# A two-layer hybrid trunk on one core: three of five gate/up pairs by seven products beside a stream of plain jobs, and half of the weight sums by adding transfers

## The chip, the core and the metric

The kernel runs on 1 core of one Trainium2 chip. The metric is device time in microseconds (us) of one execution, smaller is better; the figure compared is the median of several runs. The profile is of one execution; its engines are PE (TensorE, matmuls), PEld (its weight loads), DVE (VectorE), ACT (ScalarE), POOL (GpSimd) and SP (which here only issues transfers).

## What is computed

Two layers act on an activation of 256 rows by 1024 channels. Each layer has a mixer (retention beside a state-space scan) and a feed-forward part; only the latter is touched in what it computes:

```python
def swiglu(h, w_gate_up, w_down):          # h is 256 x 1024, after an RMS norm
    gu = h @ w_gate_up                     # 1024 x 5632
    gate, up = jnp.split(gu, [D_FF], axis=-1)     # D_FF = 2816
    return (jax.nn.silu(gate) * up) @ w_down      # 2816 x 1024
```

Inputs, weights and output are float32.

## The kernel before

**One weight piece.** Every weight arrives as a piece of 128 x 1024 numbers, 512 KB, that `feeder` (L405) loads through SP's queue into a `raw` slot, of which there are four. `split_piece` makes two operands of it: ACT copies it into `wh`, rounded to the format that the matmuls take (L421), and DVE subtracts to get the rest, `wl` (L428). `wh` and `wl` have six slots each (`hlS`). The activation is split the same way, and a product is three matmuls (`mm3`): xh·wh, xh·wl and xl·wh (L444, L445, L446). Pieces take their slots strictly in a written order (`turn`): a piece that is late holds up all that come after it.

**The feed-forward part.** Gate and up have 2816 columns each, worked on in pairs of 512 gate columns and the 512 up columns that belong to them: pairs 0 to 4, and a joint job of the last 256 columns of both. A plain pair is two jobs, gate and up, of four pieces each; a job is 8 row blocks x 2 row halves of the activation x 3 matmuls. After a job comes its evacuation: ACT takes the silu of the gate, DVE multiplies by the up part (L214, `sil<-acc,sil`), PE transposes the product (L486, `tr<-cst,sil`) and ACT and DVE split it for w_down.

**Seven products.** Pairs 2 and 4 (`WINO`) are worked as a 2 x 2 block product in Winograd's form of Strassen's scheme: rows of the activation in two halves, the 1024 inner channels in two halves, gate and up as the two column blocks. Seven products of half the size replace eight. Each is 4 x 3 matmuls, so the pair has 84 in place of 96. It needs seven weight operands of two pieces each (14 splits in place of 8). Their names are 11, t1, t2, 22, t3, 21 and t4. 11, 12, 22, 21 are the weight blocks as loaded, and

```
t1 = 11 + 12     t2 = t1 + 22     t3 = 12 + 22     t4 = t2 + 21
```

up to signs that the activation's sums and the evacuation carry. Block 11 lies in a `raws` slot (two slots, shared with the mixer's `seg`) and becomes t1, t2 and t4 there, one after another: split 11, add, split t1, add, split t2, add, split t4. Only then is the slot free. Four sums of the activation (`plain`, `D`) are made once per layer. One weight sum, t3, is made by a transfer that adds what it reads from HBM to what lies in the slot (L330, issued by POOL); the other three are DVE additions (L214, `raws<-raws,raw`), of 128 x 1024 each.

**Order.** All instructions come from a planner (`Flow`), which keeps a list per engine and issues by a number (the job) and readiness, with its own costs; the engines then run their lists strictly in order. Before, jobs stand one after another: pair 0, pair 1, pair 2, pair 3, pair 4, joint, w_down.

**Slots in the mixer.** PSUM is in three pools: `acc` with four slots, `tr` with two, `sm` with two for the mixer's small products. `ca` and `cb`, two slots each, hold the mixer's rotary and convolution halves.

Of the kernel before, what the change touches and what calls it, by code (L numbers as in the profile page):

```python
# [181 lines left out]
def trunk_kernel(  # L182
# [7 lines left out]
    WINO, ADDED = (2, 4), ("t3",)  # L190
# [49 lines left out]
    accS, new_acc = pooled(accp, (P, 512), F32, "acc", 4)  # L240
    trS, new_tr = pooled(trp, (P, 512), F32, "tr", 2)
    smS, new_sm = pooled(smp, (P, 512), F32, "sm", 2)
# [31 lines left out]
    def next_turn():  # L274
        turns.append(Event())
        return len(turns) - 1

    def add_job(srcs):
        evs = []
        for src, k, n in srcs:  # L280
            ev = Event()
            evs.append(ev)
            specs.append((src, k, n, len(jobs), (rawS, new_raw), splitter(next_turn(), k, n, ev, len(jobs))))
        jobs.append(evs)

    PRODUCTS = ("11", "t1", "t2", "22", "t3", "21", "t4")

    def add_wino(w, n1, n2):

        job = len(jobs)  # L290
        evs = {q: [Event(), Event()] for q in PRODUCTS}
        turn = {(q, i): next_turn() for q in PRODUCTS for i in range(2)}
        held = {(q, i): Event() for q in ("11", "12", "22", "21") for i in range(2)}
        part = {q: [rows(w, k0 + 2 * i * P, 2, n0, 512)[0][0] for i in range(2)]
                for q, k0, n0 in (("11", 0, n1), ("12", 0, n2), ("22", D // 2, n2), ("21", D // 2, n1))}
        for q in part:
            for i in range(2):
                land = holder(held[q, i])
                if (q, i) == ("11", 1):
                    land = then(land, [wino_sums(i, job, evs, turn, held, part) for i in range(2)])  # L300
                specs.append(([part[q][i]], 2, 512, job, (segS, new_raw_seg) if q == "11" else (rawS, new_raw), land))
        jobs.append(evs)
# [17 lines left out]
    def wino_sums(i, job, evs, turn, held, part):  # L320
# [3 lines left out]
        def split(raw, q):  # L324
            wh, wl = yield from split_piece(raw, D, turn[q, i], pr)
            fl.set(evs[q][i], tuple(a.rearrange("p (k n) -> p k n", k=2) for a in (wh, wl)))
# [7 lines left out]
        def last(raw, q, sem):  # L334
            yield from split(raw, q)
            fl.release(sem)

# [3 lines left out]
        def plus(q, x, raw, src):  # L341

            if q in ADDED:
                yield from add(x, src)
            else:
                w = yield raw
                yield tt(D, pr, x, x, w, ALU.add)
            fl.set(used[q])

        def side(ev, q, *sums):  # L350
            raw = yield ev
            yield from split(raw, q)
# [4 lines left out]
        def third():  # L357
            raw = yield w12
            if "t1" not in ADDED:
                yield used["t1"]  # L360
            yield from plus("t3", raw, w22, "22")
            yield from last(raw, "t3", rawS)

        fl.spawn(side(w22, "22", *(q for q in ("t2", "t3") if q not in ADDED)))
        fl.spawn(third())
        fl.spawn(side(w21, "21", *(q for q in ("t4",) if q not in ADDED)))
# [7 lines left out]
        yield from last(x, "t4", segS)  # L374
# [11 lines left out]
    def fm_srcs(w, n0):  # L386
        return [rows(w, k0, 4, n0, 256) for k0 in range(0, D, 4 * P)]

# [23 lines left out]
    def split_piece(raw, m, turn, pr):  # L412

        if turn:
            yield turns[turn - 1]
        yield hlS
        fl.set(turns[turn])
# [6 lines left out]
        wh = yield Op("act", 0.833 * m + 92, split_h, pr)  # L424

# [8 lines left out]
    def splitter(turn, k, n, ev, job):  # L434
        def land(raw, landed):
            yield landed
            wh, wl = yield from split_piece(raw, k * n, turn, job - 0.7)
# [62 lines left out]

    def power(ms, n, pr, tag, bufs):
# [19 lines left out]
    class Norm:  # L521


        def __init__(self, w, sums=False):
            self.plain = [[Event() if sums else None for _ in range(NT)] for _ in range(2)]
            self.ops = {q: Event() for q in PRODUCTS}
# [52 lines left out]

        def drop(self):  # L580
            for i in range(2):
                self.xT.drop(i)
            for _ in range(4):
                fl.release(bigS["D"])
# [20 lines left out]
    at_job = [0]  # L605
    started = [False]

    def tm_jobs(xT, members, order):

        first = at_job[0]  # L610
        at_job[0] += len(members)
        acc, left = {}, {}
        for m, t, k in order:
# [15 lines left out]
            yield pe(3 * mm_cost(n), j + 0.5, emit)  # L629
# [3 lines left out]
            if k == 7:  # L633
                fl.spawn(post(t, acc[m, t], j))

    def tm_job(xT, post, n=512, kper=2, lead=0):

        return tm_jobs(xT, [(post, n, kper)], [(0, t, k) for t in range(NT) for k in range(lead)]
                       + [(0, t, k) for k in range(lead, 8) for t in range(NT)])
# [6 lines left out]
    def wino_job(norm, post):  # L646
# [4 lines left out]
        j = at_job[0]  # L651
        at_job[0] += 1
        evs = jobs[j]

        def product(q, box, first):
            xh, xl = yield norm.ops[q]
            if first:
                yield accS
            for k in range(4):
                wh, wl = yield evs[q][k // 2]  # L660

                def emit():
                    if first and k == 0:
                        box.append(new_acc())
                    mm3(box[0], xh[:, k, :], xl[:, k, :], wh[:, k % 2, :], wl[:, k % 2, :], first and k == 0, k == 3,
                        skip_group_check=box is u)
# [1025 lines left out]
```

## Time and profile before

| | us |
|---|---|
| three runs | 1280.19, 1282.22, 1283.87 (median 1282.22) |
| profiled execution, its own time | 1282.07 |
| its span, first to last instruction | 1280.3 |
| outside the span | 1.8 |
| DVE busy, ACT busy in the span | 931.6, 774.5 |
| feed-forward part, layer 0 | about 467 to 586 in the span |
| feed-forward part, layer 1 | about 1097 to 1215 in the span |

In a row of the timeline stand start, length, engine, line, operation, out<-in and shape, a count for merged rows, and in brackets the idle time before it with what ended it. A matmul's length is longer than the distance to the next one, since they overlap in the array, so PE's pace is read from the starts. The same holds for DVE and ACT, whose writes end after the next instruction has begun. DMA share is the mean busy share of the core's 16 DMA engines.

### The profile page before, as it was taken

The numbers are of one execution on the slowest core, as the hardware profiler recorded it, in microseconds if no ns is written. First come the engines' busy times: TensorE is split into PE (matmuls) and PEld (weight loads), VectorE is DVE, ScalarE is ACT, GpSimd is POOL, SyncE is SP. The second block draws the span as 40 slices with busy tenths as digits, with TensorE's granted clock in tenths as the row PEclk, the third lists the DMA queues.
The fourth block names the chain that finished last, engine by engine and source line by source line (L and its number), as shares of the span: only waits on it lengthen the run. The fifth ranks groups of instructions, "written<-read, shape, count | busy, mean of one in ns | idle before, by whom it ended". The sixth has DMA issues, their size and how long they took to land.

```text
span 1280.3 us, 17056 instructions
## 1 busy us (share of the span) xinstructions
PE 1268.4 (99%) x6276; PEld 1065.7 (83%) x6276; DVE 931.6 (73%) x1243; ACT 774.5 (60%) x1138; POOL 43.1 (3%) x65
## 2 busy tenths in 40 slices
PE   9999999999999999999999999999999999999997
PEld 7888888888888888888888988888888888888886
DVE  5875789778576678995468658879875756889943
ACT  5765676977375365674367556867954643766732
POOL 1000000000010000000010000000000000000000
PEclk9999999999999999999999999999999999999999
DMA  7757555556465456766466565555555554667751
GB/s 242 221 166 221 164 185 161 181 183 212 140 223 202 161 173 188 265 206 221 157 188 202 170 201 160 185 181 179 193 182 175 203 198 148 224 169 232 242 199 53
DMA packets 131191, 241.86 MB, mean 189 GB/s; under 512 B 7946, under 2 KB 60034, under 8 KB 130979
## 3 DMA queue, kind: packets, MB, share of 16 engines
q1 hardware_dynamic: 127458, 232.16, 55.0%
q0 software_dynamic: 3648, 8.61, 3.3%
q8 instruction: 49, 0.80, 0.2%
q14 instruction: 36, 0.29, 0.1%
HBM read 239.63 MB, written 1.11 MB: 188 GB/s over the span
## 4 chain that ended last, share of the span: by engine, by line
PE 89%; DVE 4%; DMA 3%; issue 2%; ACT 2%; SPq 0%; POOLq 0%; POOL 0%; DVEq 0%; ACTq 0%
PE acc L444 21%; PE acc L446 21%; PE acc L445 21%; PE acc L740 10%; PE acc L741 6%; PE tr L486 2%; DVE wl L428 2%; PE yps L1282 2%; PE acc L743 1%; DMA raw<-in_w_gate_up_dram 1%; ACT wh L421 1%; DMA raw<-in_w_down_dram 1%; DMA raw<-in_w_in_dram 1%; PE tr L1176 1%; PE ips L1269 1%
## 5 line engine op out<-in xcount | busy, mean ns | idle before, releaser
L428 DVE TENSOR_TENSOR wl<-raw,wh 128x1024 fp32r<-128x1024 f32 (+2 forms) x424 | 503.8, 1193 | 216.8 <-ACT wh L421 214.5
L421 ACT ACTIVATE wh<-raw 128x1024 fp32r<-128x1024 f32 (+2 forms) x424 | 434.6, 1034 | 285.9 <-PE acc L446 193.0
L444 PE MATMUL acc<-wh,xT 128*128 128x512 f32 (+1 forms) x816 | 317.1, 389 | 1.0 <-ACT wh L421 0.6
L445 PE MATMUL acc<-wl,xT 128*128 128x512 f32 (+1 forms) x816 | 311.7, 382 | 0.8 <-DVE wl L428 0.7
L446 PE MATMUL acc<-wh,xT 128*128 128x512 f32 (+1 forms) x816 | 311.6, 382 | 0.0
L740 PE MATMUL acc<-xT,wh 128*128 128x512 f32 x560 | 203.6, 401 | 0.0
L444 PEld LDWEIGHTS acc<-wh,xT 128*128 128x128 f32 x816 | 153.3, 188 | 28.9 <-ACT wh L421 1.0
L445 PEld LDWEIGHTS acc<-wl,xT 128*128 128x128 f32 x816 | 153.4, 188 | 28.8 <-DVE wl L428 1.9
L446 PEld LDWEIGHTS acc<-wh,xT 128*128 128x128 f32 x816 | 153.2, 188 | 28.7
L741 PE MATMUL acc<-xT,wl 128*128 128x256 f32 x640 | 167.1, 281 | 0.0
L741 PEld LDWEIGHTS acc<-xT,wl 128*128 128x128 f32 x640 | 120.9, 189 | 6.9
L740 PEld LDWEIGHTS acc<-xT,wh 128*128 128x128 f32 x560 | 105.4, 188 | 21.4
L444 PE MATMUL acc<-wh,A 128*128 128x512 f32 x192 | 76.6, 399 | 0.0
L217 DVE SCALAR_TENSOR_TENSOR cb<-ca,cv,cb 128x255 f32<-128x255 f32 (+1 forms) x144 | 68.5, 479 | 10.9 <-ACT cb L207 9.8
L446 PE MATMUL acc<-wh,A 128*128 128x512 f32 x192 | 74.9, 390 | 0.0
L445 PE MATMUL acc<-wl,A 128*128 128x512 f32 x192 | 74.8, 389 | 0.0
L444 PE MATMUL acc<-wh,Y 128*128 128x512 f32 x176 | 70.7, 402 | 0.0
L446 PE MATMUL acc<-wh,Y 128*128 128x512 f32 x176 | 68.7, 390 | 0.0
L445 PE MATMUL acc<-wl,Y 128*128 128x512 f32 x176 | 68.5, 389 | 0.0
L421 ACT ACTIVATE wh<-raws 128x1024 fp32r<-128x1024 f32 x32 | 33.6, 1057 | 29.4 <-PE acc L446 24.8
L444 PE MATMUL acc<-wh,C 128*128 128x512 f32 x128 | 50.6, 395 | 0.0
L446 PE MATMUL acc<-wh,C 128*128 128x512 f32 x128 | 49.9, 390 | 0.0
(159 smaller groups left out, 1569.5 us busy)
## 6 DMA issues: line engine op xcount, KB each, us to landing
raw<-in_w_in_dram SPq DMA_DIRECT2D x188, 512.0 KB, 4.2
raw<-in_w_gate_up_dram SPq DMA_DIRECT2D x72, 512.0 KB, 4.7
raw<-in_w_down_dram SPq DMA_DIRECT2D x44, 512.0 KB, 3.2
raw<-in_ret_out_dram SPq DMA_DIRECT2D x32, 512.0 KB, 4.0
raw<-in_ssd_out_dram SPq DMA_DIRECT2D x32, 512.0 KB, 3.2
raw<-in_w_in_dram SPq DMA_DIRECT2D x24, 352.0 KB, 3.2
seg<-acs SPq DMA_DIRECT2D x16, 512.0 KB, 4.7
raw<-in_w_o_dram SPq DMA_DIRECT2D x16, 512.0 KB, 3.2
```

Of the source, the lines that this page charges most:

```text
L217: return Op("dve", 1.04 * n + 130, lambda: nc.vector.scalar_tensor_tensor(out=out, in0=in0, scalar=scalar, in1=in1, op0=op0, op1=op1), pr)
L421: nc.scalar.activation(out=wh[:, :m], in_=raw[:, :m], func=AF.Copy)
L428: nc.vector.tensor_tensor(out=wl[:, :m], in0=raw[:, :m], in1=wh[:, :m].bitcast(F32), op=ALU.subtract)
L444: nc.tensor.matmul(ps, lhsT=lh, rhs=rh, start=first, stop=False, **kw)
L445: nc.tensor.matmul(ps, lhsT=lh, rhs=rl, start=False, stop=False, **kw)
L446: nc.tensor.matmul(ps, lhsT=ll, rhs=rh, start=False, stop=last, **kw)
L486: nc.tensor.transpose(out=ps[:, j * P : (j + 1) * P], in_=src[:, j * P : (j + 1) * P], identity=ident)
L740: nc.tensor.matmul(a, lhsT=wh[:, k % 4, fsl], rhs=x[:, k % 4, :, :], start=k == 0, stop=False)
L741: nc.tensor.matmul(a[:, :SEQ], lhsT=wl[:, k % 4, fsl], rhs=xh[:, k % 4, :], start=False, stop=False)
L743: nc.tensor.matmul(a, lhsT=wh[:, k % 4, fsl], rhs=x[:, k % 4, :, :], start=False, stop=True)
L1176: nc.tensor.transpose(out=tps[:, (2 * t + b) * P : (2 * t + b + 1) * P], in_=sT[:, b, t * P : (t + 1) * P], identity=ident)
L1282: nc.tensor.matmul(ps[:, i * HD : (i + 1) * HD], lhsT=sg[:, i, :], rhs=xdt[:, i * HD : (i + 1) * HD], start=True, stop=True)
```

## The change

Pairs 2, 3 and 4 go by seven products instead of pairs 2 and 4. They run as one stream, in the order 2, 3, 4, beside a second stream of plain jobs: pair 1's gate, pair 1's up, and the joint job. The order of a seven-product pair (`ASIDE`) has four places (`*`) for a piece of the other stream, so 14 splits of a pair alternate with 4 plain pieces. t4 joins t3 as a sum by adding transfer; t1 and t2 stay with DVE. Block 12 lies in a `cc` slot instead of a `raw` slot. `cc` is the former `ca` and `cb` in one tile of 1024; the small products' two PSUM slots join `acc`, which has six. The evacuation of the seven products is rewritten so that it ends in the plain jobs' own functions (`gate_post`, `up_post`). `W_SSD`, `W_DOWN` and `APART` are code paths that stay switched off. Outside the feed-forward parts the instructions are the same in number, and their order differs at a handful of places by one or two rows.

```diff
-    WINO, ADDED = (2, 4), ("t3",)
+    APART = ()
+    W_SSD, W_DOWN = False, False
...
-    accp = ctx.enter_context(tc.tile_pool(name="accp", bufs=4, space=PSUM))
+    accp = ctx.enter_context(tc.tile_pool(name="accp", bufs=6, space=PSUM))
...
-    smp = ctx.enter_context(tc.tile_pool(name="smp", bufs=2, space=PSUM))
...
-    caS, new_ca = pooled(tp, (P, 2, SEQ), F32, "ca", 2)
-    cbS, new_cb = pooled(tp, (P, 2, SEQ), F32, "cb", 2)
+    ccS, new_cc = pooled(tp, (P, D), F32, "cc", 2)
...
+    ASIDE = ("11", "*", "t1", "*", "t2", "22", "*", "t3", "*", "21", "t4")
+    ALONE = ("11", "t1", "t2", "22", "t3", "21", "t4")
...
+    FFN = [[("plain", 0)],
+           [("seven", (2, 3, 4), ("t3", "t4")), ("plain", 1, NPAIR)]]
...
+        for i, members in enumerate(FFN):
+            if i == 0:
+                yield from tm_pair(ffn.xT, *((m, 512, 2) for m in pair(members[0][1])))
+            else:
+                pe_pr = at_job[0]
+                yield from together(*[ffn_jobs(take(n_jobs(*m)), pe_pr, *m) for m in members])
```

Three places of the order, all in layer 0; layer 1 has the same. The first is SP's list of loads of gate and up weights. Before, after pair 0 and pair 1 (16 pieces), with `raws` for block 11 of a seven-product pair:

```order
L405 DMA raw<-in_w_gate_up_dram 128x2x512 x16
L405 DMA raws<-in_w_gate_up_dram 128x2x512 x2
L405 DMA raw<-in_w_gate_up_dram 128x2x512 x14
L405 DMA raws<-in_w_gate_up_dram 128x2x512 x2
L405 DMA raw<-in_w_gate_up_dram 128x2x512 x6
L405 DMA raw<-in_w_gate_up_dram 128x2x256 x8
```

After (the last plain pieces, the joint job's, are two transfers of 256 KB each):

```order
L458 DMA raw<-in_w_gate_up_dram 128x2x512 x8
L458 DMA raws<-in_w_gate_up_dram 128x2x512 x2
L458 DMA raw<-in_w_gate_up_dram 128x2x512
L458 DMA cc<-in_w_gate_up_dram 128x2x512 x2
L458 DMA raw<-in_w_gate_up_dram 128x2x512 x7
L458 DMA raws<-in_w_gate_up_dram 128x2x512 x2
L458 DMA raw<-in_w_gate_up_dram 128x2x512
L458 DMA cc<-in_w_gate_up_dram 128x2x512 x2
```

Between two loads of `raws` stood 14 others, eight of them a plain pair's; now the ten others are the same pair's own and its four plain pieces', and the next `raws` load waits for the t4 split of the pair before it.

The second is DVE's list between pair 0's activation sums (`plain`, `D`) and pair 0's first evacuation (`sil<-acc,sil`), for which PE's transposes wait. Before:

```order
L214 TENSOR_TENSOR D<-plain,D 128x4x128
L428 TENSOR_TENSOR wl<-raw,wh 128x1024
L214 TENSOR_TENSOR plain<-plain 128x512
L428 TENSOR_TENSOR wl<-raw,wh 128x1024
L214 TENSOR_TENSOR D<-plain,D 128x4x128
L428 TENSOR_TENSOR wl<-raw,wh 128x1024
L214 TENSOR_TENSOR plain<-plain 128x512
L428 TENSOR_TENSOR wl<-raw,wh 128x1024 x2
L214 TENSOR_TENSOR D<-plain,D 128x4x128
L214 TENSOR_TENSOR sil<-acc,sil 128x512 x2
```

After:

```order
L214 TENSOR_TENSOR D<-plain,D 128x4x128
L499 TENSOR_TENSOR wl<-raws,wh 128x1024
L214 TENSOR_TENSOR plain<-plain 128x512
L214 TENSOR_TENSOR raws<-raws,cc 128x1024
L214 TENSOR_TENSOR D<-plain,D 128x4x128
L499 TENSOR_TENSOR wl<-raws,wh 128x1024
L214 TENSOR_TENSOR plain<-plain 128x512
L499 TENSOR_TENSOR wl<-raw,wh 128x1024
L214 TENSOR_TENSOR D<-plain,D 128x4x128
L499 TENSOR_TENSOR wl<-raws,wh 128x1024
L214 TENSOR_TENSOR sil<-acc,sil 128x512 x2
```

Five operations of 128 x 1024 stand there in both; the `raw` pieces of pair 1 have given way to `raws` pieces of pair 2 and a sum.

The third is DVE's list from the first t4 split of pair 2 over the border to pair 3, in the changed kernel (before has no such border: a plain pair stands between two seven-product pairs). The first row's two splits are t4 of pair 2; the next `wl<-raws` rows are block 11 of pair 3, from freshly loaded slots:

```order
L499 TENSOR_TENSOR wl<-raws,wh 128x1024 x2
L214 TENSOR_TENSOR sx<-acc,sx 128x512
L499 TENSOR_TENSOR wl<-raws,wh 128x1024
L214 TENSOR_TENSOR sx<-acc,sx 128x512
L499 TENSOR_TENSOR wl<-raws,wh 128x1024
L499 TENSOR_TENSOR wl<-raw,wh 128x1024
L214 TENSOR_TENSOR raws<-raws,cc 128x1024 x2
L214 TENSOR_TENSOR sil<-sx,sil 128x512
L499 TENSOR_TENSOR wl<-raws,wh 128x1024 x2
L214 TENSOR_TENSOR raws<-raws,raw 128x1024
L499 TENSOR_TENSOR wl<-raw,wh 128x1024
```

There it goes on with a sum, t2, 22 and t2 again. Two evacuation rows, five splits, two sums and one more evacuation row stand between the load of `raws` and the first sum that makes t2.

More of the change, by code (lines that the diff above doesn't have):

```diff
@@ L272, in trunk_kernel @@
     turns = []
[L274 to L302, printed above, removed]
@@ L318, in then, with wino_sums, split @@
         return run
-    def wino_sums(i, job, evs, turn, held, part):
+    def wino_sums(i, job, evs, turn, held, part, added, zS):
         pr = job - 0.7
-        def split(raw, q):
-            wh, wl = yield from split_piece(raw, D, turn[q, i], pr)
+        def split(raw, q, src=None):
+            wh, wl = yield from split_piece(raw, D, turn[q, i], pr, src)
             fl.set(evs[q][i], tuple(a.rearrange("p (k n) -> p k n", k=2) for a in (wh, wl)))
@@ L351, in side @@
             raw = yield ev
-            yield from split(raw, q)
+            yield from split(raw, q, part[q][i] if q in added else None)
             for a in sums:
```

552 lines of the change are left out of this document (369 added, 183 removed).

## The prediction

> **What bounds the kernel now.** I read the page first. Its parts 1, 2 and 3 carry these lines:
>
> ```profile
> PE 1268.4 (99%) x6276; PEld 1065.7 (83%) x6276; DVE 931.6 (73%) x1243; ACT 774.5 (60%) x1138; POOL 43.1 (3%) x65
> PEclk9999999999999999999999999999999999999999
> q1 hardware_dynamic: 127458, 232.16, 55.0%
> q0 software_dynamic: 3648, 8.61, 3.3%
> ```
>
> PE is busy for 99% of the span at a granted clock that is full in every slice, so time can only come from fewer matmuls or from waits. Next, PE's pace, in the timeline of pair 0's up job (columns: start, length, instruction; in brackets the idle time before it):
>
> ```profile
> 480.74 0.39 PE L445 MATMUL acc<-wl,xT 128*128 128x512 f32 x1
> ...
> 485.05 0.39 PE L446 MATMUL acc<-wh,xT 128*128 128x512 f32 x1
> 485.74 0.66 PE L486 MATMUL tr<-cst,sil 128*128 128x128 f32 x4 [0.30 <-DVE sil L214]
> 486.15 0.47 PE L444 MATMUL acc<-wh,xT 128*128 128x512 f32 x1
> ```
>
> Between the first two rows lie 19 distances in 4.31 us: a matmul of 128x512 costs 0.227 us. Four transposes cost 0.41 (485.74 to 486.15). They start 0.69 after the last matmul where pace would be 0.23: 0.46 us of PE lost. At the same place in layer 1:
>
> ```profile
> 1114.91 0.39 PE L446 MATMUL acc<-wh,xT 128*128 128x512 f32 x1
> 1116.16 0.66 PE L486 MATMUL tr<-cst,sil 128*128 128x128 f32 x4 [0.86 <-DVE sil L214]
> ```
>
> Here 1.25 - 0.23 = 1.02 us are lost. The busy table by windows shows the two feed-forward parts (columns: window, length, then busy time of PE, PEld, DVE, ACT, POOL with counts, clock, DMA share, GB/s):
>
> ```profile
> 467.60:586.00 118.40, 117.88 (x545) 97.06 (x544) 105.39 (x111) 77.65 (x94) 5.48 (x5) 1.00 0.72 224
> 1097.50:1215.00 117.50, 116.32 (x536) 95.32 (x535) 104.16 (x109) 76.96 (x92) 5.47 (x5) 1.00 0.71 221
> ```
>
> PE is full there too, but DVE stands at 89% and the DMA engines at 0.72. This is the stage with the least to spare, and the change loads just these two.
>
> **The matmuls removed.** Pairs 1 and 3 were plain before. Now pair 1 still is, and pair 3 goes from 96 matmuls of 128x512 to 84. That is 12 per layer, 24 in all: 24 x 0.227 = 5.45 us, all on the path, since PE is what is always busy. The Trainium skill ("TensorE: Matmul & The Clock Gate", Part 1) gives 512 columns at 2.4 GHz plus about 2.5 ns, 215.7 ns from start to start; by it the term would be 5.18 us. The trace differs, with 227 ns.
>
> **What DVE, ACT and the transfers get.** DVE's dense pace, from its timeline:
>
> ```profile
> 563.23 2.35 DVE L428 TENSOR_TENSOR wl<-raws,wh 128x1024 fp32r<-128x1024 f32 x2
> 565.50 0.68 DVE L214 TENSOR_TENSOR sx<-acc,sx 128x512 f32<-128x512 f32 x1
> 566.10 1.22 DVE L428 TENSOR_TENSOR wl<-raw,wh 128x1024 fp32r<-128x1024 f32 x1
> 567.24 0.68 DVE L214 TENSOR_TENSOR sx<-acc,sx 128x512 f32<-128x512 f32 x1
> ```
>
> Starts give 1.14 us per split (1.22 long when alone) and 0.60 per operation of 512. Per layer DVE gets six more splits and about four more of 512: 6 x 1.14 + 4 x 0.60 = 9.2 us. Its sums stay at twelve (two pairs by three before, three pairs by two now). The group view of the `raws` tiles has the rest:
>
> ```profile
> L421 ACT ACTIVATE wh<-raws x32: 1042/1061/1066, 493.8 to 1193.1; 128x1024 fp32r<-128x1024 f32 x32
> L214 DVE TENSOR_TENSOR raws<-raws,raw x24: 1218/1224/1227, 496.1 to 1191.6; 128x1024 f32<-128x1024 f32 x24
> ```
>
> A sum is as long as a split, so 1.14 when dense; ACT's copy is 1.06. After, the stretch in which the two streams run holds 3 x 84 + 96 + 48 = 396 matmuls, 89.9 us, and about 4 of transposes: 94 us of PE. DVE has 42 + 12 = 54 splits and 12 sums, 75.2 us, and some 30 operations of 512, 18: about 93.5. ACT, with 54 copies at 1.06 and its evacuations, stays at about 70% and I cost it at nothing. DVE fits with half a microsecond to spare and lives on its lead: it enters the stretch ahead of PE by the six `wh`/`wl` slots, and I cost its added work at nothing where the lead lasts. If the lead goes, every idle moment of DVE becomes PE's.
>
> Transfers: q1's 55.0% of 1280.3 us over 232.16 MB is 1.59 us of all 16 engines per 512 KB. The eight adding transfers of before:
>
> ```profile
> L330 POOL DMA_DIRECT2D raw<-in_w_gate_up_dram x8: 1194/1207/1275, 497.9 to 1175.1; - x8
> DMA to landing us min/median/max: 5.9/5.9/6.1
> ```
>
> and two of them by themselves, in the transfer view of 497.5 to 507 (9.5 us):
>
> ```profile
> q0 software_dynamic: 544, 1.05, 68.0%
> ```
>
> 68% of 9.5 us for two is 3.2 us of all engines each, twice a load. The stretch holds 36 loads and 12 adds: 36 x 1.59 + 12 x 3.2 = 96 us by the mean, or 36 x 1.37 + 38 = 87 by the quickest queued loads (next fence), in 94. Where before put loads and adds together, the engines were full already:
>
> ```profile
> 535.00:550.00 15.00, 15.00 (x68) 12.43 (x67) 13.01 (x12) 7.46 (x8) 2.98 (x3) 1.00 0.99 287
> ```
>
> yet PE lost nothing there (15.00 busy of 15.00). The rule of the Trainium skill that speaks against this change ("DMA: Bandwidth & Descriptors", Queues, on arbitration) is that an engine goes round between its queue rows packet by packet, so an add takes its turn against a load; the price is rival C's.
>
> **The wait that goes.** Why PE waited for pair 0's transposes stands in the chain of waits:
>
> ```profile
> 477.33 4.73 DMA raw<-in_w_gate_up_dram
> 482.16 1.07 ACT wh L421
> 483.25 0.90 DVE wl L428
> 484.40 0.68 DVE D L214
> 485.08 0.61 DVE sil L214
> 485.74 0.66 PE tr L486 x4
> ...
> 1107.19 5.28 DMA raw<-in_w_gate_up_dram
> 1112.58 1.07 ACT wh L421
> ```
>
> A `raw` load of pair 1 came late into its slot, and DVE, strictly in order, held `sil` back behind that piece's split. After, most of the pieces ahead of `sil` are `raws` and a sum with `cc`, whose slots are free early and don't wait for `raw`; DVE's work there is equal, five operations of 1024. So I count the 0.46 + 1.02 = 1.48 us as gone. Bounds: 0 (one `raw` piece still stands there) to 1.48 saved. What is late next is DVE itself, whose last two operations before the transposes remain, and PE has other work for about that long.
>
> **The border waits that come.** Twice per layer (pairs 2 to 3, 3 to 4) block 11 of the next pair reloads the `raws` slots right after the t4 splits. Queued behind its first split on DVE are its sums and all splits of the pair. Before had a plain pair in that place, so no row shows this wait; I bound it by loads. One that is alone, two and two that queue, and seven that queue:
>
> ```profile
> L405 SPq DMA_DIRECT2D raw<-in_w_gate_up_dram x3: 368/368/368, 524.7 to 529.4; - x3
> DMA to landing us min/median/max: 3.4/3.4/3.4
> ...
> L405 SPq DMA_DIRECT2D raws<-in_w_gate_up_dram x2: 464/507/550, 531.6 to 532.1; - x2
> DMA to landing us min/median/max: 4.5/5.9/6.9
> ...
> L405 SPq DMA_DIRECT2D raw<-in_w_gate_up_dram x5: 367/368/368, 477.3 to 484.5; - x5
> L405 SPq DMA_DIRECT2D raws<-in_w_gate_up_dram x2: 461/462/462, 483.0 to 483.5; - x2
> DMA to landing us min/median/max: 4.6/5.7/7.8
> ```
>
> The four of the second query (two `raw`, two `raws`, issued from 531.2 to 532.9) landed 1.37 us apart; the seven of the third 1.71 apart. Now the walk, with PE's end of the piece six slots ahead of t4 as zero. A hop 0.3 (an estimate; the hop from a load to ACT in the chain is 482.16 - 482.06 = 0.1), ACT 1.06, DVE 1.22: t4's first split ends at 2.6. Load 3.4: lands at 6.0. ACT 1.06 and a hop 0.1: `wh` at 7.2. PE needs it after the six slots' 45 matmuls, 10.2; `wl` follows at 8.4, needed at 10.4: hidden, 2.0 to spare, and in the 4.6 us between DVE has its evacuation rows. From 8.4 on DVE is dense: twelve more splits and sums, 13.7, and two operations of 512, 1.2, to t2's second `wl` at 23.3. PE needs that after 100 matmuls and four transposes: 22.7 + 0.4 = 23.1. So 0.2 us late with landings 1.37 apart, and 0.8 with 1.71: I take 0.5 between them. At the border from 3 to 4 the adds of t4 share the engines with the loads (they go out after t2's splits, have about 7.6 us to land, and take 5.9 alone); I take 1.0, from 0.2 to 2.5 (0.8, and half of one add's 3.2 more, rounded up). Per layer 1.5, in all 3.0; bounds 0.8 to 6.6.
>
> The pooled PSUM and `cc` slots I cost at nothing: six slots either way, and the mixer's rows stay as they were but for a few.
>
> **The sum.** Against the profiled execution's own 1282.07: -5.45 - 1.48 + 3.0 = -3.9, so 1278.1. The three runs before have their median at 1282.22, 0.15 above the profiled one: no difference that matters. 0.3% is 3.85 us, about what a measurement of this kernel can tell from no change; the forecast lies on that line.
>
> **Rivals.** A: the border waits hide wholly. A plain piece's twelve matmuls give 2.7 us of PE for 1.14 of DVE, so each `*` renews the lead. Then 1282.07 - 5.45 - 1.48 = 1275.1. For it: 535 to 550, full engines without a wait. Against: DVE's half microsecond to spare. The Trainium skill ("Perfetto Trace Analysis", Optimization Strategy) says that interleaving regimes with different busiest engines may help; no run shown bears on it yet.
>
> B: the refill comes at the slow rate at every border, and pair 0's wait stays in part: four borders at 1.6 (0.8 and half a load's 1.59) are 6.4, so 1282.07 - 5.45 - 1.48 + 6.4 = 1281.5, no change. For it: 96 us of transfers in 94.
>
> C, the slower side: the adds of t4 land late behind the loads, so that t4's splits come late, the `raws` reload after them too, and the lead of DVE is gone when the border comes. Each border then shows the 3.2 us of a whole add and one split, 1.14: 4.3, and four of them 17.2: 1275.1 + 17.2 = 1292.3. It decides from (5.45 + 1.48 + 3.85) / 4 = 2.7 us per border. For it: a share of 0.99 where adds and loads met. Against: PE lost nothing there. That the change doesn't take the matmuls out is no rival: the lists have 84 in place of 96.
>
> **Chances.** A 0.25, forecast 0.40, B 0.20, C 0.15. The forecast sits on the 0.3% line, so half of it counts as faster, half as same: faster 0.25 + 0.20 = 0.45, same 0.20 + 0.20 = 0.40, slower 0.15. The range takes in A, the forecast and B: from 1274.0 (A, and 1 us for single waits elsewhere) to 1284.0 (B, and the border bound 6.6 with nothing saved at pair 0: 1282.07 - 5.45 + 6.6 = 1283.2, rounded up); C lies outside.
>
> **What would show it.** Page, part 1: PE at x6252. The timeline: starts 0.227 apart, and no wait ahead of pair 0's transposes; if it is there, the 1.48 is wrong. At the borders, waits of PE for `wl` or `wh` that sum to about 1.5 us per layer; none means A, over 2.7 each with adds landing in 8 us or more means C. DVE near 99% in the stretch; if DVE idles far from a border while PE waits for it, the lead account is wrong and so is the forecast.

## The result and the profile after

The changed kernel takes 1300.71 us (median of four runs, 1299.94 to 1303.94) against 1283.05 before: a ratio of 1.0146, 95% interval 1.0122 to 1.0171. It is 18 us slower. The forecast was 1278.1, in a range to 1284.0, with faster the likeliest and 0.15 for slower.

The page of the changed kernel, parts 1 to 3:

```profile
PE 1271.7 (98%) x6252; PEld 1063.4 (82%) x6252; DVE 947.7 (73%) x1263; ACT 786.4 (61%) x1156; POOL 61.3 (5%) x81
PEclk9999999999999999999999999999999999998999
q1 hardware_dynamic: 127458, 232.16, 56.0%
q0 software_dynamic: 8000, 17.00, 7.0%
```

The 24 matmuls are gone (x6252), the loads are what they were (232.16 MB), and the adding transfers went from 8 to 24 (their queue from 8.61 to 17.00 MB). The span grew by 19.0 us, from 1280.3 to 1299.3, with fewer matmuls in it: PE waits. I add up, over PE's starts in a feed-forward part, what exceeds 0.227 us per matmul and 0.10 per transpose; where the part is taken to end, and which small distances count, moves such a sum by up to a microsecond. Before, that is 1.7 us in layer 0 and 2.7 in layer 1; after, 13.7 and 14.5. So 23.8 us of waits came and 5.45 of matmuls went: 18.4.

The waits sit in three places, the same in both layers. The first is the border from pair 2 to 3, in PE's timeline:

```profile
515.91 0.50 PE L516 MATMUL acc<-wl,xT 128*128 128x512 f32 x1 [0.34 <-DVE wl L499]
...
518.08 0.50 PE L516 MATMUL acc<-wl,xT 128*128 128x512 f32 x1 [0.50 <-DVE wl L499]
...
519.82 0.50 PE L516 MATMUL acc<-wl,xT 128*128 128x512 f32 x1 [0.76 <-DVE wl L499]
```

With the transposes at 522.8 this is 2.4 us beyond pace (2.5 in layer 1). The second is the border from pair 3 to 4:

```profile
544.24 0.39 PE L517 MATMUL acc<-wh,xT 128*128 128x512 f32 x1
547.70 1.09 PE L557 MATMUL tr<-cst,sil 128*128 128x128 f32 x4 [3.07 <-DVE sil L214]
548.44 0.78 PE L515 MATMUL acc<-wh,xT 128*128 128x512 f32 x1
549.01 0.63 PE L516 MATMUL acc<-wl,xT 128*128 128x512 f32 x1
549.44 0.63 PE L517 MATMUL acc<-wh,xT 128*128 128x512 f32 x1
549.87 0.63 PE L515 MATMUL acc<-wh,xT 128*128 128x512 f32 x1
...
551.12 0.39 PE L515 MATMUL acc<-wh,xT 128*128 128x512 f32 x1
551.35 0.39 PE L516 MATMUL acc<-wl,xT 128*128 128x512 f32 x1
```

A wait of 3.07, and behind it matmuls that start 0.43 apart in place of 0.227, until 551.1. With the small waits around it, 5.0 us in layer 0 and 5.8 in layer 1. The third place is behind pair 4: waits of 1.76 ahead of a matmul at 581.9 and of 0.93 and 0.41 ahead of transposes at 591.5 and 597.9, 3.6 us beyond pace (3.5 in layer 1):

```profile
581.92 0.50 PE L515 MATMUL acc<-wh,xT 128*128 128x512 f32 x1 [1.76 <-ACT sil L207]
...
591.54 0.44 PE L557 MATMUL tr<-cst,sil 128*128 128x128 f32 x2 [0.93 <-DVE A L214]
...
597.89 0.66 PE L557 MATMUL tr<-cst,sil 128*128 128x128 f32 x4 [0.41 <-DVE C L214]
```

The rest, some 5.4 us over both layers, is in waits of under 0.35 us.

Why the second wait is there stands in the chain of waits of the changed kernel:

```profile
532.88 9.10 DMA raw<-in_w_gate_up_dram
542.27 0.76 issue
543.03 0.58 ACT sil L207
543.61 0.95 ACT wh L477
544.63 1.11 issue
545.74 1.22 DVE wl L499
546.95 0.61 DVE sil L214
547.70 1.09 PE tr L557 x4
...
569.36 8.99 DMA raw<-in_w_gate_up_dram
578.43 1.07 ACT wh L477
```

A load of 512 KB took 9.10 us. It is the second piece of block 21. ACT and DVE take pieces strictly in order: that piece, then the two t4 splits, then the evacuation `sil`, for which PE's transposes wait. A second such load (8.99) stands ahead of the third place. What ran beside the load is in the view of the adding transfers issued from 529 to 534, and of SP's loads in the same stretch:

```profile
L380 POOL DMA_DIRECT2D raws<-in_w_gate_up_dram x2: 1194/1198/1203, 529.7 to 532.0; - x2
...
DMA to landing us min/median/max: 8.0/8.9/9.8
```

```profile
L458 SPq DMA_DIRECT2D raw<-in_w_gate_up_dram x2: 368/368/368, 530.6 to 532.9; - x2
...
DMA to landing us min/median/max: 7.4/8.3/9.1
```

The adds of t4 and the loads of 21 go out 0.9 us apart (529.75 and 530.61, 532.02 and 532.88), and each load lands when the add beside it does. This agrees with the rule of the Trainium skill ("DMA: Bandwidth & Descriptors", Queues, on arbitration) that a DMA engine takes turns between queue rows by packets. The busy table of the changed kernel shows what the DMA engines did meanwhile (the last three columns are the clock, the DMA share and GB/s):

```profile
533.00:541.00 8.00, 8.00 (x37) 6.58 (x36) 6.15 (x7) 3.67 (x4) 0.22 (x1) 1.00 1.03 244
541.80:545.80 4.00, 2.58 (x11) 1.48 (x9) 2.43 (x3) 3.73 (x5) 0.00 (x0) 1.00 0.00 0
545.00:550.00 5.00, 2.30 (x8) 2.04 (x9) 4.90 (x7) 2.13 (x4) 0.00 (x0) 0.77 0.58 185
```

From 533 to 541 they are full; in the 4 us after, they carry nothing, because SP's next load in order is a `raws` load that waits for t4's split, and every load after it waits with it. Full and idle come in turns at both borders (from 506.0 to 509.5 the share is 0.00 too): from one pair's first `raws` load (509.54) to the next pair's (545.85) are 36.3 us, where PE's work in one of the three pairs with its plain pieces is 31.3 (94 over three). The third row shows the clock after PE's wait: 0.77.

### The profile page after: what moved, and what is told of

The parts are those of the page before. It is cut to its first block, busy times and chain, and to the rows that moved or that the text cites. A ratio compares the mean times of both kernels' runs of the same rounds, so it can differ in the third digit from the quotient of the medians.

```text
span 1299.3 us, 17111 instructions
## 1 busy us (share of the span) xinstructions
PE 1271.7 (98%) x6252; PEld 1063.4 (82%) x6252; DVE 947.7 (73%) x1263; ACT 786.4 (61%) x1156; POOL 61.3 (5%) x81
## 3 DMA queue, kind: packets, MB, share of 16 engines
q1 hardware_dynamic: 127458, 232.16, 56.0%
## 4 chain that ended last, share of the span: by engine, by line
PE 80%; DVE 7%; DMA 7%; issue 3%; ACT 2%; SPq 0%; DVEq 0%; POOLq 0%; POOL 0%; ACTq 0%
PE acc L515 18%; PE acc L516 18%; PE acc L517 18%; PE acc L898 10%; PE acc L899 6%; DMA raw<-in_w_gate_up_dram 5%; DVE wl L499 5%; PE yps L1491 2%; PE tr L557 2%; PE acc L901 1%; ACT wh L477 1%; DMA raw<-in_w_in_dram 1%; DVE raws L214 1%; DMA raw<-in_w_down_dram 1%; PE tr L1385 1%
## 5 line engine op out<-in xcount | busy, mean ns | idle before, releaser
L499 DVE TENSOR_TENSOR wl<-raw,wh 128x1024 fp32r<-128x1024 f32 (+2 forms) x408 | 483.5, 1191 | 219.0 <-ACT wh L477 216.7
L477 ACT ACTIVATE wh<-raw 128x1024 fp32r<-128x1024 f32 (+2 forms) x408 | 417.2, 1033 | 283.5 <-PE acc L517 181.6
L515 PE MATMUL acc<-wh,xT 128*128 128x512 f32 (+1 forms) x776 | 302.4, 390 | 4.7 <-ACT sil L207 3.5
L516 PE MATMUL acc<-wl,xT 128*128 128x512 f32 (+1 forms) x776 | 298.5, 385 | 4.4 <-DVE wl L499 4.3
L517 PE MATMUL acc<-wh,xT 128*128 128x512 f32 (+1 forms) x776 | 297.4, 383 | 0.0
L516 PEld LDWEIGHTS acc<-wl,xT 128*128 128x128 f32 x776 | 146.7, 189 | 34.5 <-DVE wl L499 8.7
L515 PEld LDWEIGHTS acc<-wh,xT 128*128 128x128 f32 x776 | 146.9, 189 | 32.8 <-ACT sil L207 4.9
L517 PEld LDWEIGHTS acc<-wh,xT 128*128 128x128 f32 x776 | 146.6, 189 | 27.5 <-DVE xT L214 0.4
L217 DVE SCALAR_TENSOR_TENSOR cc<-cc,cv 128x255 f32<-128x255 f32 (+1 forms) x144 | 68.4, 478 | 11.0 <-ACT cc L207 9.8
L477 ACT ACTIVATE wh<-raws 128x1024 fp32r<-128x1024 f32 x48 | 50.0, 1055 | 28.9 <-DVE raws L214 17.1
L499 DVE TENSOR_TENSOR wl<-raws,wh 128x1024 fp32r<-128x1024 f32 x48 | 57.6, 1218 | 7.8 <-ACT wh L477 7.6
L557 PE MATMUL tr<-cst,sil 128*128 128x128 f32 x280 | 42.1, 279 | 9.9 <-DVE sil L214 6.3
```

What stands on the lines that cost most here:

```text
L217: return Op("dve", 1.04 * n + 130, lambda: nc.vector.scalar_tensor_tensor(out=out, in0=in0, scalar=scalar, in1=in1, op0=op0, op1=op1), pr)
L477: nc.scalar.activation(out=wh[:, :m], in_=raw[:, :m], func=AF.Copy)
L499: nc.vector.tensor_tensor(out=wl[:, :m], in0=raw[:, :m], in1=wh[:, :m].bitcast(F32), op=ALU.subtract)
L515: nc.tensor.matmul(ps, lhsT=lh, rhs=rh, start=first, stop=False, **kw)
L516: nc.tensor.matmul(ps, lhsT=lh, rhs=rl, start=False, stop=False, **kw)
L517: nc.tensor.matmul(ps, lhsT=ll, rhs=rh, start=False, stop=last, **kw)
```

## The experiments

All changes are made to the changed kernel. Theory T is that transfers make the waits, the rival R that the reload of the `raws` slots behind t4 makes them. The kernel before took 1282.3 to 1283.2 us beside these runs. "Waits" are the two layers' sums beyond pace in the profiled execution, worked out as above: 28.2 us in the changed kernel, 4.4 before.

**t4 by copies in place of adds.** The sum t4 is left out.

```diff
-                out=raw.rearrange("p (k n) -> p k n", k=2), in_=part[q][i], accum_op=ALU.add), pr)
+                out=raw.rearrange("p (k n) -> p k n", k=2), in_=part[q][i],
+                **({} if q == "21" else {"accum_op": ALU.add})), pr)
```

> This kernel is the changed one with every instruction in the same place, but t4's two transfers per pair overwrite the slot and add nothing (t4 is then 21 alone; the sum is left out). A copy of 512 KB takes about 1.4 us of the 16 engines, an add about 3.1 (its queue's share grew from 3.3% of 1280.3 us to 7.0% of 1299.3 us over 16 more adds: 48.7 / 16 = 3.0). Theory T (the engines are the bound once t1 and t2 are split: four adds and four loads, some 18 us, have to go through in about 20, and t4 and the loads of 21 beside it land late): 2 x 1.7 = 3.4 us less per pair, so the 3.07 us wait ahead of the transposes at the border from 3 to 4 (547.7) and the 1.76 us one at the end of pair 4 (581.9) go, with the half-clock matmuls behind the first: 1282 to 1289 us. Rival R (the reload of the raws slots behind t4's splits, with SP's other loads held behind it, makes the wait whatever the transfers cost): the waits at the borders stay, 1297 to 1301.

Measured: 1290.48 us, ratio 1.0061 (1.0046 to 1.0076), waits 19.0. Every instruction stands where it stood, so the adding itself costs 10 of the 18 us. The two transfers at the same place land sooner:

```profile
L380 POOL DMA_DIRECT2D raws<-in_w_gate_up_dram x2: 742/748/753, 527.4 to 529.7; - x2
...
DMA to landing us min/median/max: 6.7/6.7/6.8
```

6.7 in place of 8.0 and 9.8. The 3.07 us wait became 1.43 in layer 0 and 0.53 in layer 1, not nothing: the result lies between the two theories.

**t4 left out altogether**: its split reads the slot as t2 left it, with no transfer and no sum.

```diff
-            if q in added:
+            if q == "t4":
+                pass
+            elif q in added:
```

> t4 is neither added nor copied: its split reads the slot as t2 left it (the sum is left out), so two transfers per pair are gone altogether. The copies of the run before still took 1.4 us each of the engines and gave 10 us back of the 18. If the transfers are all that is left (theory T), another 2 x 1.4 = 2.8 us per pair of engine time and the landing itself go: 1277 to 1284 us. If the reload of the raws slots behind t4's splits is what is left (theory R), the waits for wl right after the border (551.4 and 552.7 in the copy run, 1.9 us together) stay, and so do those ahead of the joint job's transposes at the end (1.1): 1286 to 1290.

Measured: 1281.66 us, ratio 0.9989 (0.9978 to 1.0000), waits 8.8. So t4's twelve transfers cost 19.0 us in all, 8.8 as transfers of any kind and 10.2 by adding, which is the whole loss. It closes the sum, too: 1282.86 - 5.45 + (8.8 - 4.4) = 1281.8. The matmuls' gain is real, and 4.4 us more of waits than before are left without any of t4's transfers. With pair 0's wait gone, the borders and the pairs behind them show about 5.9 us (2.3 in layer 0, 3.6 in layer 1). The other slots, below, take these away, so they come with the reload.

**t4 as DVE sums.** `("t3", "t4")` becomes `("t3",)`.

> t4 is a DVE sum again in all three pairs, the two streams stay. Adds per pair go from four to two (6.2 us of the engines less), DVE gets 2 x 1.14 = 2.3 us more per pair. Theory T: t4 no longer waits for transfers, so the waits at the borders shrink below 1 us each; what is left is DVE, which needs 93.5 + 6.8 = 100 us in a stretch of 94: up to 6 us per layer less the lead of 2 to 5, so 1279 to 1287 us. Rival R (the reload): each border still shows its 2 to 3 us and DVE's added work comes on top: 1294 to 1302.

Measured: 1286.25 us, ratio 1.0024 (1.0007 to 1.0042), waits 13.8, none of them over 1.1 us, most of them for `wl`. As T said. The loads of 21, with no add beside them, now land in 3.6 us:

```profile
L458 SPq DMA_DIRECT2D raw<-in_w_gate_up_dram x2: 368/368/368, 528.5 to 530.8; - x2
...
DMA to landing us min/median/max: 3.6/3.6/3.6
```

What limits now is in its busy table:

```profile
520.00:550.00 30.00, 28.70 (x126) 22.55 (x125) 29.23 (x30) 18.43 (x20) 1.74 (x2) 1.00 0.70 200
550.00:585.00 35.00, 32.42 (x146) 25.35 (x145) 33.76 (x36) 25.93 (x32) 3.02 (x3) 1.00 0.75 226
```

DVE is 97% busy (29.23 of 30, 33.76 of 35) and the DMA engines at 0.70 and 0.75: the bound went from the transfers to DVE.

**Pair 3 in the other slots**: 11, t1, t2, t4 in `cc`, 12 and t3 in `raws`.

```diff
+            xS, new_x = first or (segS, new_raw_seg)
...
-                                               slots=(ccS, new_cc)) for c in at[0])))
+                                               slots=((ccS, new_cc), (segS, new_raw_seg))[i % 2],
+                                               first=((segS, new_raw_seg), (ccS, new_cc))[i % 2]) for i, c in enumerate(at[0]))))
```

> Pair 3 has its block 11 (and t1, t2, t4) in the two cc slots and its block 12 (and t3) in the two raws slots; pairs 2 and 4 stay. cc is free after t3's split, before t4's, so block 11 of the next pair can load before t4 of the pair at hand is split; the adds are as many and as costly as before. Rival R (the reload makes the waits): the border waits go, 1278 to 1285 us. Theory T (late adds): the border from 2 to 3 gets its 2 to 3 us back, but t4 still lands 8 to 10 us after issue and DVE still holds the evacuations behind its splits; block 12 now waits for t4 in place of block 11: 1290 to 1299.

Measured: 1292.49 us, ratio 1.0076 (1.0056 to 1.0097), waits 19.6: in T's range, but 8 us better than the changed kernel. So the reload has a part. At the border from 3 to 4 no wait of PE is left, neither the 3.07 nor its slow matmuls. At the border from 2 to 3, where now block 12 reloads the `raws` slots behind t4, one wait of 2.00 stands in place of three short ones, with slow matmuls behind it:

```profile
516.15 0.39 PE L516 MATMUL acc<-wh,xT 128*128 128x512 f32 x1
518.54 0.70 PE L517 MATMUL acc<-wl,xT 128*128 128x512 f32 x1 [2.00 <-DVE wl L500]
519.03 0.63 PE L518 MATMUL acc<-wh,xT 128*128 128x512 f32 x1
519.46 0.63 PE L516 MATMUL acc<-wh,xT 128*128 128x512 f32 x1
```

Behind pair 4 waits of 1.77 and 1.17 remain.

**The other slots with copies, without t4, and with DVE sums.** Three combinations of the edits above; the first two leave out the sum t4.

> t4 by copies (the sum is left out) and pair 3 in the other pair of slots: both suspected costs are cut at once. They gave 10 and 8 us alone. If the two are separate and add up, 1280 to 1284 us; if they are one chain (a slot's round of load, splits, adds, split, load), whose length both cut, the second gives little: 1287 to 1291.

> Neither add nor copy for t4 (its sum is left out) and pair 3 in the other pair of slots. If t4's transfers (19 us in the run without them) and the reload of the slots behind t4 (7 to 8 us in both runs with the other slots) are all there is, their sum leaves the matmuls' gain: 1274 to 1277 us. If DVE's 93.5 us in 94 are a third limit, or the refilled border was only hidden by the transfers, 1279 to 1283.

> t4 as DVE sums and pair 3 in the other slots, the computation whole. The run with DVE sums alone gave 1286; its waits are for wl. If they come from the reload, 7 us go: 1278 to 1281. If they come from DVE's 100 us in a stretch of 94, they stay: 1284 to 1288.

Measured: 1283.01 with copies (ratio 0.9998, 0.9988 to 1.0008), 1283.39 without t4 (0.9998, 0.9988 to 1.0008), 1285.93 with DVE sums (1.0027, 1.0016 to 1.0038). With copies the other slots still give 7.5 us, in the range that was put for two costs that add up; without t4's transfers they give nothing (1281.66 to 1283.39), nor with DVE sums (1286.25 to 1285.93). So the reload tells most when t4 is late. My reading of the swapped kernel without t4, that the two costs would add up to 1274 to 1277, failed. Its waits show why: at the borders none over 0.1 us are left, so the 5.9 us of the reload are gone, but 3.2 us per layer came at the transposes behind pair 4 and at the matmul after them. They stand in the swapped runs with adds and with copies too, and not in the run without t4's transfers in the first slots: here the swap gives and takes about the same. With DVE sums a wait of 3.23 stands at 539.3 in place of theirs.

**No streams**: whole jobs in the order pair 0, seven 2, pair 1, seven 3, joint, seven 4.

> No streams: whole jobs in the order pair 0, seven 2, pair 1, seven 3, joint, seven 4, with t3 and t4 as adds. If running two streams is what costs, this gives the 5.45 us of the matmuls: 1275 to 1279 us. Theory T: a seven-product pair by itself has 84 x 0.227 = 19 us of PE beside eight loads and four adds, 8 x 1.4 + 4 x 3.1 = 23.6 us of the engines, so each of the three stands 2 to 5 us longer unless the plain job ahead has paid in advance; 6 to 15 us per layer: 1287 to 1305.

Measured: 1295.08 us, ratio 1.0092 (1.0071 to 1.0114), in T's range; waits 19.0, in the fastest of the four executions (1290.34). The loss doesn't need the interleaving: 12 of the 18 us are there without it. Its chain of waits in layer 0 runs through an add of t4, issued at 492.90 and 8.35 long, to a wait of PE at 503.88.

**Two seven-product pairs in the stream**, pair 3 plain again: `(2, 4)` beside `("plain", 1, 3, NPAIR)`.

> The stream with pairs 2 and 4 alone by seven products, beside pairs 1 and 3 and the joint job as plain jobs, t3 and t4 as adds: the matmuls of the kernel before (5.45 us more than the changed kernel), one border between seven-product pairs per layer in place of two. If the losses sit at the borders and behind each pair's t4, as the trace shows them (2.4 and 5 to 6 us at the two borders, 3.5 at the end, per layer), one border of the first kind and the end remain, twice 5 to 7 us: 1291 to 1296. If the third pair as such is what cannot be fed, 1282 to 1285.

Measured: 1301.24 us, ratio 1.0143 (1.0125 to 1.0161), waits 24.6. Both expectations missed: 20.2 us of waits came without the third pair, 23.8 with it, and there are 5.45 us more of matmuls. The longest wait stands behind the second pair, where no third reloads the slots:

```profile
548.37 1.09 PE L557 MATMUL tr<-cst,sil 128*128 128x128 f32 x4 [3.08 <-DVE sil L214]
```

A load of 9.29 us, issued at 533.36, stands ahead of it in the chain. So this wait, as long as the 3.07 of the changed kernel, belongs to t4's adds and the loads beside them, and not to the reload at a border.

**One of t4's two pieces by DVE.** `added = added if i else ("t3",)` in `wino_sums`: the second piece stays an add.

> Of t4's two pieces one is a DVE sum and one an add by transfer, in all three pairs: three adds per pair in place of four, DVE 1.14 us more per pair. Theory T with DVE as the second limit: the engines lose 3.1 us per pair, t4's first piece is at hand early, DVE needs 96.9 us in 94: between the run with both on DVE (1286) and less, 1281 to 1286. If only DVE were the limit, 1293 (half way from 1300.7 to 1286); if only the transfers, about the same.

Measured: 1295.66 us, ratio 1.0096 (1.0076 to 1.0116), waits 25.0. T's number missed, and so did the other two. One add per pair is enough: it lands 7.9 us after issue, beside a load of 21 as before, and waits of 1.5 us at pair 3's evacuation and 3.6 at pair 4's remain.

**The fourth plain piece behind block 21**: `"t3", "21", "*", "t4"` ends the order.

> The fourth plain piece of a unit moves from ahead of block 21 to behind it, so that PE and DVE have one more plain piece, 2.7 us of PE, between t4's adds and t4's splits. Theory T (t4 lands late): up to 2.7 us less at each of three places per layer, 1287 to 1294 us. Rival R (the reload after t4 sets the border): t4's splits come no earlier, and the evacuation has one piece less to hide behind: 1299 to 1304.

Measured: 1306.78 us, ratio 1.0177 (1.0160 to 1.0194), waits 35.1. Above both ranges. More time for t4 made it worse, and not for R's reason: now a plain piece's load is the one that lands beside the add (8.8 us), and PE waits for it at 542.6 (1.56, for `wh`).

**t4 summed by POOL** from block 21's `raw` slot, alone and with the other slots.

```diff
-            if q in added:
+            if q == "t4":
+                w = yield raw
+                yield pool(D, pr, x, x, w, ALU.add)
+            elif q in added:
...
-           [("seven", (2, 3, 4), ("t3", "t4")), ("plain", 1, NPAIR)]]
+           [("seven", (2, 3, 4), ("t3",)), ("plain", 1, NPAIR)]]
```

> t4 is summed by POOL from the raw slot that block 21 is loaded into, neither a DVE sum nor a transfer, the computation whole. POOL is busy 5% of the time; no trace shows its speed on 128 x 1024, the planner books 2.3 us. If late transfers and DVE's load are the two costs, this avoids both, and leaves the reload: like the run without the sum, 1281 to 1285. If POOL's work slows DVE beside it or is over 4 us itself, 1288 to 1296.

> The sum by POOL and pair 3 in the other slots, the computation whole: all three costs avoided. If the account holds, 1274 to 1279 us, below the kernel before; if POOL's sums are slow or hold DVE up, 1282 to 1292.

Measured: 1305.60 us (ratio 1.0172, 1.0158 to 1.0186) and 1311.03 (1.0217, 1.0195 to 1.0240), above all ranges. The group view of the first, and DVE's timeline beside the two sums from 535.7 to 545.4:

```profile
L227 POOL TENSOR_TENSOR raws<-raws,raw x12: 3015/3376/6430, 498.4 to 1222.0; 128x1024 f32<-128x1024 f32 x12
```

```profile
540.38 2.82 DVE L502 TENSOR_TENSOR wl<-raw,wh 128x1024 fp32r<-128x1024 f32 x1
543.12 2.82 DVE L214 TENSOR_TENSOR sil<-sx,sil 128x512 f32<-128x512 f32 x1
```

A sum takes POOL 3.0 to 6.4 us, and a split that takes DVE 1.22, and an operation of 512 that takes 0.68, took 2.82 each; the DVE operations beside the sums before 540 kept their length. POOL spans are rough. This way of adding is no cure.

**t3 without its adds**: its split reads block 12 as loaded, the sum t3 is left out.

> t3 is neither added nor copied (its split reads block 12 as loaded, the sum is left out), t4's adds are as in the changed kernel, both DVE chains too. Theory Q (the two t3 adds just ahead in POOL's queue and on the engines push t4's adds and the loads of 21 back): t4's adds land about 6 us after issue in place of 8 to 10 and the wait ahead of the transposes shrinks from 3.1 to under 1: 1282 to 1288 us. Theory L (an add's own landing, 6 us by itself, sits in the slot's round and is what is too long): most of the wait stays, 1292 to 1297.

Measured: 1299.53 us, ratio 1.0133 (1.0115 to 1.0151), not told apart from the changed kernel's 1.0146. Theory Q fell: half of all adds gone, and nothing gained; the time is above L's range too, and nearer to it. The views of t4's adds and of SP's loads in the same stretch:

```profile
L380 POOL DMA_DIRECT2D raws<-in_w_gate_up_dram x2: 1194/1196/1197, 529.0 to 531.3; - x2
...
DMA to landing us min/median/max: 7.5/8.4/9.2
```

```profile
L460 SPq DMA_DIRECT2D raw<-in_w_gate_up_dram x2: 368/368/368, 529.9 to 532.1; - x2
...
DMA to landing us min/median/max: 6.9/7.7/8.6
```

Two adds and two loads by themselves still take until 7.5 and 9.2 us after each add's issue. By the forecast's prices they are 2 x 3.2 + 2 x 1.4 = 9.2 us of the DMA engines, and they take 11.7 from the first issue (529.0) to the last landing (540.7).

**t3 as a DVE sum, t4 by adds**: `("t4",)`.

> t3 becomes a DVE sum, t4 stays an adding transfer, the computation whole: two adds per pair in place of four, DVE with 2.3 us more per pair, as in the run with t4 on DVE (1286). Theory Q: only the number of adds counts, so 1284 to 1289 us. Theory L: t4's adds still sit in the slot's round, and DVE's added work comes on top: 1295 to 1303.

Measured: 1313.78 us, ratio 1.0241 (1.0216 to 1.0267). As many adds as with t4 on DVE (1286.25) and 27.5 us slower: which sum is the add decides, not how many are. It is above L's range as well; why t3 on DVE costs 13 us more than t3 by adds stays open.

**Block 21's product first**, and then the plain piece ahead of t4 in place of behind 21.

```diff
-    ASIDE = ("11", "*", "t1", "*", "t2", "22", "*", "t3", "*", "21", "t4")
+    ASIDE = ("21", "*", "11", "*", "t1", "*", "t2", "22", "*", "t3", "t4")
...
+    ASIDE = ("21", "11", "*", "t1", "*", "t2", "22", "*", "t3", "*", "t4")
```

> Block 21's own product, which waits for no sum, moves from ahead of t4 to the head of each pair, with a plain piece behind it; the computation is whole, adds and DVE work as in the changed kernel. Block 21's loads then no longer run beside t4's adds, and at a border three splits that need no raws slot stand ahead of block 11's. If the loss is t4's adds sharing the engines with the loads of 21 in a round that has no slack (9 to 10 us for two adds and two loads), and the reload behind it, most of the 18 us come back: 1279 to 1287 us. If an add of 6 us or more in the slot's round is too long whatever stands beside it, 1292 to 1300.

> As the run above, but the plain piece stands between t3 and t4 in place of behind 21: t4's adds have one more piece (2.7 us of PE) to land, the border one less to hide behind. If t4's landing is what is left, 1 to 4 us faster than the run above; if the reload is, or the plain piece's load is late beside the adds as in the run with the plain piece behind 21, 2 to 6 slower.

Measured: 1288.70 us (ratio 1.0049, 1.0036 to 1.0061), waits 15.0, and 1288.96 (1.0056, 1.0043 to 1.0070). Twelve of the 18 us are back, with all adds in place, a little short of the range for it; the plain piece's place makes no difference, against both readings of it. t4's adds of the first kernel, at the same border:

```profile
L380 POOL DMA_DIRECT2D raws<-in_w_gate_up_dram x2: 1194/1198/1203, 530.1 to 531.8; - x2
...
DMA to landing us min/median/max: 6.0/7.2/8.3
```

The first lands in 6.0, in place of 8.0; the second, with a load issued 0.9 us behind it (532.65, landing in 7.7), in 8.3. This order does two things, it parts the adds from 21's loads and it puts splits that need no `raws` slot at the border; how the 12 us divide was not tried.

**The same with t4's second piece as a DVE sum.** `added = ("t3",) if i else added`.

> As the run with block 21's product at the head (1288.7), but of t4's two pieces the second is a DVE sum; the computation is whole. There the first add lands in 6.0 us and the second, queued behind it, in 8.3, and the border's reload waits for the second. If that queue is what remains, the second piece by DVE brings the border 2 us forward, four times, against 1.1 us of DVE per pair: 1280 to 1285 us. If DVE, now 96.9 us in a stretch of 94, is what remains, 1288 to 1292.

Measured: 1282.78 us, ratio 0.9998 (0.9986 to 1.0009), waits 10.3. This fits the reading that the queue of two adds was what remained; that half of t4's adds are gone at the same time isn't told apart from it. This version, the computation whole, equals the kernel before; no whole version here beats it.

## Why the prediction was wrong

- **The matmuls, -5.45: right.** PE has 24 fewer, and the sum for the kernel without t4's transfers closes with that number.
- **Pair 0's wait, -1.48: right.** In the changed kernel's PE timeline the transposes stand without a wait:

```profile
485.70 0.60 PE L557 MATMUL tr<-cst,sil 128*128 128x128 f32 x4
```

- **The border waits, +3.0: the step that failed.** It was put as "they go out after t2's splits, have about 7.6 us to land, and take 5.9 alone", and 1.0 was taken for it. 5.9 is the time of an add with no load issued beside it. Here they took 8.0 and 9.8, and the loads of 21 issued with them, which stand ahead of t4 in the strict order, took 7.4 and 9.1. The forecast's own prices were a warning: two adds and two loads are 2 x 3.2 + 2 x 1.4 = 9.2 us of the DMA engines, where an add has 7.6, and the second, issued 2.3 later, until 9.9. The reload was put too low as well, at 0.5 a border, 2.0 in all: some 5.9 us are there without t4's transfers. The two borders came to 2.4 and 5.0 in layer 0, 2.5 and 5.8 in layer 1, where 0.5 and 1.0 stood.
- **A third place was left out.** Behind pair 4 there is no `raws` reload, so the walk did not look there; but t4's splits hold up the evacuation and the joint job there too, 3.6 and 3.5 us.
- **What follows a wait was left out.** After the long waits PE ran at half pace: 16 distances of 0.39 to 0.43 in place of 0.227, 3.1 us over both layers.
- **The transfers' sum, 87 to 96 us in 94, asked the wrong question.** It came out near its lower end: from 480 to 582 the share is 0.84, 86 us of 102, some loads for w_down among them. But in the stretch the share went from 1.03 to 0.00 within ten microseconds. A mean near one, with a chain in it that has to wait for its end, gives stalls, not a fit.
- **DVE's half microsecond to spare (75.2 + 18 is 93.2, so 0.8) was not the limit**: from 525 to 545 it was busy 16.45 of 20 us. It became the limit where t4 was summed by DVE.
- **Rival C was the case**, by its mechanism and close to its price: 4.3 us per border were forecast, 2.4 to 5.8 measured. The four borders come to 15.7 us (17.2 were forecast); the third place's 7.1 and small waits make up the difference from 1292.3 to 1300.7. C got 0.15 because PE had lost nothing where the DMA engines stood at 0.99 before. That row could not speak for t4. The adds there were t3's, and leaving t3's adds out gains nothing in the changed kernel either. And loads and adds stood in it one behind the other more than beside each other, as SP's loads of 535 to 550 and POOL's timeline of the kernel before show:

```profile
L405 SPq DMA_DIRECT2D raw<-in_w_gate_up_dram x3: 368/368/368, 534.6 to 538.2; - x3
...
DMA to landing us min/median/max: 5.6/6.2/6.7
```

```profile
541.63 1.19 POOL L330 DMA_DIRECT2D raw<-in_w_gate_up_dram  x1 [39.35 <-DMA raw<-in_w_gate_up_dram]
544.03 1.19 POOL L330 DMA_DIRECT2D raw<-in_w_gate_up_dram  x1 [1.20 <-DMA raw<-in_w_gate_up_dram]
```

The last of the loads landed at 543.8 (538.2 + 5.6), and the two adds in 5.9 and 6.1, as all eight of that kernel did: no load was issued beside one.

What stays open is how the 12 us of the order with block 21 first divide, and why the waits of the stream with only two such pairs are nearly those of the one with three.

## What to carry to other kernels

Moving a sum from an engine to an adding transfer is free only if nobody stands behind its landing: ask what the sum's result releases, and price the landing with what is issued in the same microseconds, not alone. Add up DMA engine time inside the window between issue and need, not over the whole stage. If such a transfer must stand in a slot's round, put the pieces that don't depend on it between it and the need, and load them earlier.

## What the runs showed of the hardware

- A load that is issued 0.9 us after an add on another queue lands with it, at 7.4 and 9.1 us, where a load alone takes 3.4 (before) and 3.6 (t4 as DVE sums).
- After PE waits of 3.07 us (changed kernel) and 2.00 us (pair 3 in the other slots) matmuls started 0.43 us apart for 2 to 4 us; after one of 1.76 they did not. The Trainium skill ("TensorE: Matmul & The Clock Gate", Part 1) gives 426.7 ns for 512 columns on the slow clock, and the 0.43 agrees; it speaks of an idle window of about 3.4 us, and here 2.00 was enough.
- The length of a wait alone does not decide it. In the run without t3's adds a wait of 1.87 us in layer 0 was followed by the slow pace and one of 3.02 was not; with t3 by DVE one of 3.08 was not. The granted clock of the changed kernel is 0.50 from 547.65 to 551.07 and from 1185.95 to 1192.77, stretches of 3.41 us and twice that. Laid on from such a stretch in steps of 3.41 (582.24 to 585.65 in the run without t3's adds), the 3.02 (543.39 to 546.41) falls into two of them, 1.3 and 1.7 us, and the 1.87 into one.
- A copy issued by POOL kept it for 0.75 us, an adding transfer 1.20.
- Beside sums by POOL two DVE operations per pair, of 1.22 or 0.68 us by themselves, took 2.8 to 3.4; others beside them did not.
